# A hybrid S5 and Hyena encoder on one core: laying out and loading the constants and first spectra of the inverse transform anew

## The chip, the cores and the metric

The kernel runs on one core of one Trainium2 chip. The metric is the device time of one execution in microseconds; the median of three runs before the change is 1438.66 us (1438.37 to 1439.34). The trace is one profiled execution, and every start time below counts from its first instruction. TensorE (PE in the trace; PEld is its weight load), VectorE (DVE), ScalarE (ACT), GpSimd (POOL) and SyncE (SP) each run their own list of instructions in order; SP, ScalarE and GpSimd also issue the transfers (DMAs), and an issue that waits holds up what is behind it on that engine.

## The reference

One residual layer on `x` (1 x 1024 x 1024, float32): RMSNorm, one wide input projection, two token mixers side by side (a bidirectional S5 scan and a Hyena operator), a gated merge, an output projection, a residual add and a last RMSNorm. The change lies in the Hyena part:

```python
sc = conv_b
for j in range(HY_SHORT):
    sc = sc + pp[:, j:j + L] * conv_w[j]
v, x1, x2 = jnp.split(sc, HY_ORDER + 1, axis=-1)
kf = hyena_filters(L, w1, b1, freq, w2, b2, w3, decay)
z = v.astype(f32)
for o, g in enumerate((x1, x2)):
    zf = jnp.fft.rfft(z, n=2 * L, axis=1)
    conv = jnp.fft.irfft(zf * kf[:, o][None], n=2 * L, axis=1)[:, :L]
    z = g.astype(f32) * (conv + d[o].astype(f32) * z)
```

Everything is computed to float32 precision. TensorE gets it by splitting each operand in a high and a low part and adding three products (high-high, low-high, high-low).

## The kernel before, in words

The transforms are matmuls with constant matrices. Each of the two orders (o = 0, 1) has a way out and a way back.

The way out (`forward`, called through `fwd_pools`) takes four groups of 256 channels (cq). For each group it makes spectra for four frequency blocks, in the order jj = 0, 2, 1, 3: matmuls with the constants `zc` and `z0` into PSUM, sums and differences `ke` and `x` on VectorE, products `m` with the filter's spectrum `kt` (loaded by SP, two buffers) on VectorE, and a store to the scratch tensor `d_y` in device memory (`emit`, L775, issued by ScalarE).

The way back (`inverse`, L630) handles 128 channels at a time, eight times. For each it needs four spectra (j = 0, 2, 1, 3), each loaded back to a raw tile `yraw` by SP (`spectrum`, L621), split by ScalarE (high part, a cast) and VectorE (low part, a subtraction) into a tile `y`, and then 48 matmuls against the constants `ic` (high and low, four blocks each) and `icp` (the padded first block). ScalarE copies half of the PSUM result to `isn`, VectorE makes `pm` from both halves. In the first way back (`hy_inverse0`) GpSimd multiplies `pm` with a gate and forms a sum and a difference (L836 to L840), TensorE transposes the result (`store`, `to_time`), and it is stored for the second way out. There is one PSUM accumulator for it, so an inverse can't begin before the last one's result has been read.

Between the inverses TensorE works on projections of the normalised input. For the gates of the first way back there are eight, `x1(0)` to `x1(7)`: five are put ahead of the first inverse, and run among the matmuls of the last way out; the other three are cut in thirds (`proj_thirds`) and dealt between the inverses by the tuple (1, 2, 1, 1, 1, 2, 1, 0). Each projection's weights are loaded raw by SP (L508), cast and negated by ScalarE, and completed by a transfer of GpSimd that adds (L512).

Tiles live in pools, and pools are stacked from a left and a right end of the on-chip memory. When a pool is closed its room is given to the next one opened there; the first writer of a new tile then waits for the last reader of every old tile that its own tile overlaps. On the right side, above the gates, the way out has `fw_c` (`zc` 24 KB and `z0` 2 KB per partition), then `fw_w` (both `kt` 4 KB each, `eo2` 2 KB, `z` 16 KB) and `fw_t` (`m` 8 KB, then three tiles of 4 KB for `ke` and `x`). The way back has there `iv_c` (two `ic` tiles of 16 KB, `icp` 2 KB), and then the raw spectra, `y`, `isn` and `pm`. On the left, past the normalised input, lie three tiles `fv` of 4 KB, read by the transposes ahead of the way out. `load_ic` issues all nine loads on SP, ahead of the spectra.

The order on each engine is made by a planner that follows the program's order as priority and simulates when each instruction would be ready; `issue_after(i)` puts the instructions of a block behind instruction `i` on that instruction's engine, and `high_priority` moves them forward. Each inverse is put behind the last matmul of the projection before it (`self.summed`), each third behind the last matmul of an inverse (`self.rotated`).

Of the kernel before, what the change touches and what calls it, by code (L numbers as in the profile page):

```python
# [9 lines left out]
F = mybir.dt.float32  # L10
R = mybir.dt.float32r
# [89 lines left out]
class Trunk:  # L101
# [503 lines left out]
            V.tensor_tensor(out=o[:, 1], in0=self.minus(t), in1=self.minus(g), op=ALU.mult)  # L605
            V.tensor_tensor(out=z, in0=t[:, 0:1], in1=g[:, 0:1], op=ALU.mult)

    def load_ic(self, cp):
        nc, I = self.nc, self.staged
        self.ic = [cp.tile([128, 4, 1026], R, name=f"ic{i}") for i in range(2)]  # L610
        self.ic0 = cp.tile([128, 512], R, name="icp")
        nc.sync.dma_start(out=self.ic0.bitcast(F), in_=I["c_ic0"])
        for j in (0, 2, 1, 3):
            for i, sfx in enumerate(("hi", "lo")):
                nc.sync.dma_start(out=self.ic[i][:, j].bitcast(F), in_=I["c_ic_" + sfx][:, j])

    def inverse_start(self, o):
        self.iv_todo = [(o, cq, ct, j) for cq in range(4) for ct in range(2) for j in (0, 2, 1, 3)]
        self.iv_ready = []

    def spectrum(self):  # L621
        o, cq, ct, j = self.iv_todo.pop(0)
        raw = self.iv_r.tile([128, 2, 2, 128], F, name="yraw")
        self.nc.sync.dma_start(out=raw.rearrange("p a b c -> p (a b) c"),
                               in_=self.d_spec[o][cq, j][:, :, ct * 128:ct * 128 + 128])
        y = self.iv_y.tile([128, 2, 2, 2, 128], R, name="y")
        self.split(raw, y[:, 0], y[:, 1])
        self.iv_ready.append(y)

    def inverse(self, pi):  # L630

        nc = self.nc
        ps = pi.tile([128, 2, 512], F, name="iv")
        for nj, j in enumerate((0, 2, 1, 3)):
            while len(self.iv_ready) < self.iv_ahead and self.iv_todo:
                self.spectrum()
            y = self.iv_ready.pop(0)
            for par in range(2):
                for pqi in range(2):
                    cols, dst = (((slice(0, 258), ps[:, 0, 0:258]), (slice(514, 770), ps[:, 0, 256:512])),  # L640
                                 ((slice(258, 514), ps[:, 1, 0:256]),
                                  (slice(770, 1026), ps[:, 1, 256:512])))[par][pqi]
                    for a, b in ((0, 0), (0, 1), (1, 0)):
                        lhsT = y[:, a, par, pqi]
                        first = nj == 0 and pqi == 0 and a == 0 and b == 0
                        last = nj == 3 and pqi == 1 and a == 1
                        if first and par == 0:
                            nc.tensor.matmul(out=ps[:, 0], lhsT=lhsT, rhs=self.ic0, start=True, stop=False)
                        else:
                            self.rotated = nc.tensor.matmul(out=dst, lhsT=lhsT, rhs=self.ic[b][:, j, cols], start=first, stop=last)  # L650
        while len(self.iv_ready) < self.iv_ahead and self.iv_todo:
            self.spectrum()
        s = self.iv_w.tile([128, 2, 256], F, name="isn", bufs=1)
        nc.scalar.copy(out=s, in_=ps[:, :, 256:512])
        pm = self.iv_w.tile([128, 2, 512], F, name="pm")
        for a, op in enumerate((ALU.add, ALU.subtract)):
            nc.vector.tensor_tensor(out=pm[:, a].rearrange("p (b q) -> p b q", b=2), in0=ps[:, :, 0:256], in1=s, op=op)
        nc.vector.tensor_copy(out=pm[:, 0, 0:1], in_=ps[:, 0, 0:1])
        nc.vector.tensor_copy(out=pm[:, 1, 0:1], in_=s[:, 0, 0:1])
        return pm  # L660
# [96 lines left out]
    def fwd_pools(self, ctx, o):  # L757

        tc, nc = self.tc, self.nc
        mk = lambda n, b, **kw: ctx.enter_context(tc.tile_pool(reuse_waits="tile", name=f"{n}{o}", bufs=b, side="right", **kw))  # L760
        cp, wp, tp = mk("fw_c", 1), mk("fw_w", 1), mk("fw_t", 3)
        self.pf = mk("fw_p", 4, space=PSUM)
        self.load_zc(cp)
        self.d_spec[o] = self.dram.tile([4, 4, 128, 4, NCH], F, name=f"d_y{o}")

        class Pools:
            @staticmethod
            def tile(shape, dt, name, tag=None, bufs=None):
                if tag == "t4":
                    return tp.tile(shape, dt, name=name, tag=tag)  # L770
                if tag == "t8":
                    return tp.tile(shape, dt, name=name, tag=tag, bufs=1)
                return wp.tile(shape, dt, name=name, bufs=bufs)

        def emit(cq, jj, y):  # L775
            nc.scalar.dma_start(out=self.d_spec[o][cq, jj], in_=y.rearrange("p a b c -> p (a b) c"))

        return wp, lambda cq, z: self.forward(o, cq, z, Pools, self.pf, lambda jj, y: emit(cq, jj, y))

    def inv_pools(self, ctx, o, ny):  # L780
        tc = self.tc
        mk = lambda n, b, **kw: ctx.enter_context(tc.tile_pool(reuse_waits="tile", name=f"{n}{o}", bufs=b, side="right", **kw))
        self.load_ic(mk("iv_c", 1))
        self.iv_r, self.iv_y, self.iv_w = mk("iv_r", ny[0]), mk("iv_y", ny[1]), mk("iv_w", 2)
        self.iv_ahead = ny[1]

    def hy_v(self):

# [32 lines left out]
    def hy_inverse0(self):  # L821

        tc, nc = self.tc, self.nc
        self.d_z1 = self.dram.tile([4, 128, 2, 2048], F, name="d_z1")
        with ExitStack() as ctx:
# [2 lines left out]
            pi = ctx.enter_context(tc.tile_pool(reuse_waits="tile", name="iv_p", bufs=1, space=PSUM, side="right"))  # L828
            pt = ctx.enter_context(tc.tile_pool(reuse_waits="tile", name="iv_pt", bufs=2, space=PSUM, side="right"))
            gates, back = {}, {}  # L830
            self.inverse_start(0)

            def rotate(c):
                g = gates.pop(c)
# [13 lines left out]
            def x1(c):  # L848
                def use_x1(ps):
                    g = self.gates[c % len(self.gates)]  # L850
                    self.fold(self.conv(ps, 8 + c, "cv"), None, g)
                    gates[c] = g.rearrange("p a b c d -> p a (b c d)")
                return 16 + c, use_x1

            for c in range(5):
                self.proj(*x1(c))
            thirds = (t for c in range(5, 8) for t in self.proj_thirds(*x1(c)))
            for c, n in enumerate((1, 2, 1, 1, 1, 2, 1, 0)):
                with tc.issue_after(self.summed.ins):
                    rotate(c)  # L860
                if c:
                    store(c - 1)
                with tc.issue_after(self.rotated.ins):
                    for _ in range(n):
                        next(thirds)
# [470 lines left out]
    def inverse_tail(self, ctx):  # L1336

        self.inv_pools(ctx, 1, (6, 4))
        self.inverse_start(1)
        self.iv_p = ctx.enter_context(self.tc.tile_pool(reuse_waits="tile", name="iv_p1", bufs=2, space=PSUM, side="right"))  # L1340

    def hy_inverse1(self, zh, zl):
# [173 lines left out]
```

## Time and profile before

| what | us |
|---|---|
| median of three runs | 1438.66 |
| the profiled execution | 1442.31 |
| its span, first to last instruction | 1440.2 |
| TensorE busy | 1347.0 (94%) |
| VectorE busy | 1012.9 (70%) |
| ScalarE busy | 516.1 (36%) |
| GpSimd busy | 398.3 (28%) |

A matmul counts as busy from its start to its modelled end, and matmuls overlap, so a busy TensorE is not one at its peak; an idle one is idle. The first way out ends and the first way back begins between 840 and 900 us; the second pair does so between 1110 and 1170 us. Those two stretches, and the waits in them, are what the change touches.

### The profile page before, as it was taken

To read this page: it belongs to the slowest core of one execution; us is meant where nothing else is said; L and a number is where in the kernel's file an instruction comes from. 1 tells how busy PE (TensorE), PEld (TensorE's weight loads), DVE (VectorE), ACT (ScalarE), POOL (GpSimd) and SP (SyncE) were. 2 spreads that over 40 slices of the span, in tenths; PEclk is the share of its full clock that TensorE was granted. 3 is DMA by queue.
4 is the path that set the end of the run, shared out by engine and by line. 5 is a ranking of instruction groups with operands and counts; after the bars stand their busy time and mean duration, and the time that the engine had idled before them with its cause. 6 is when DMAs were issued, how large, how long until landed. Compare 5 with 4: busy or idle time off the path is not lost.

```text
span 1440.2 us, 19526 instructions
## 1 busy us (share of the span) xinstructions
PE 1347.0 (94%) x7219; PEld 1133.2 (79%) x7219; DVE 1012.9 (70%) x1938; ACT 516.1 (36%) x737; POOL 398.3 (28%) x331
## 2 busy tenths in 40 slices
PE   5888999999999999999999983999999989999997
PEld 3777798888888877887788873998888768978886
DVE  7999997698689878224499994663898734743632
ACT  5576663223323332442322221443222224522322
POOL 3766775000000001132112100553022223332222
PEclk8898999999999999999999996999999999999999
DMA  8221225864794644567965658569787897766331
GB/s 275 92 75 74 81 116 135 207 159 132 200 272 113 135 122 95 150 166 200 327 188 166 185 168 263 176 205 306 235 273 249 261 262 228 212 181 155 130 111 68
DMA packets 188619, 257.24 MB, mean 179 GB/s; under 512 B 23069, under 2 KB 144153, under 8 KB 185788
## 3 DMA queue, kind: packets, MB, share of 16 engines
q1 hardware_dynamic: 149212, 153.69, 34.4%
q0 software_dynamic: 11520, 39.85, 14.6%
q10 hardware_dynamic: 27792, 62.45, 12.1%
q8 instruction: 57, 0.93, 0.3%
q14 instruction: 38, 0.31, 0.1%
HBM read 147.49 MB, written 76.82 MB: 156 GB/s over the span
## 4 chain that ended last, share of the span: by engine, by line
PE 63%; DVE 15%; DMA 9%; issue 2%; ACT 1%; POOL 1%; SPq 0%; ACTq 0%; DVEq 0%; POOLq 0%
PE pps L556 38%; PE ops L1417 6%; PE iv L650 5%; DMA yraw<-d_y 3%; DMA zc<-c_zc_lo_d 2%; PE po L404 2%; PE pps L536 2%; PE fwo L701 2%; DMA d_y<-x 2%; PE pe L414 1%; PE fwe L701 1%; DVE st L1249 1%; DVE st L1247 1%; PE zt L686 1%; DMA ic<-c_ic_lo_d 1%
## 5 line engine op out<-in xcount | busy, mean ns | idle before, releaser
L512 POOL DMA_DIRECT2D wlo<-wraw x76 | 66.2, 871 | 709.1 <-ACT wlo L511 523.0
L556 PE MATMUL pps<-xh,whi 128*128 128x512 f32 x848 | 216.6, 403 | 4.0 <-DVE cv L581 4.0
L556 PE MATMUL pps<-xl,whi 128*128 128x512 f32 x848 | 212.5, 397 | 0.0
L556 PE MATMUL pps<-xh,wlo 128*128 128x512 f32 x848 | 210.1, 396 | 0.0
L556 PEld LDWEIGHTS pps<-xh,whi 128*128 128x128 f32 x848 | 159.9, 192 | 41.4 <-ACT wlo L511 3.6
L556 PEld LDWEIGHTS pps<-xh,wlo 128*128 128x128 f32 x848 | 157.9, 188 | 36.8
L556 PEld LDWEIGHTS pps<-xl,whi 128*128 128x128 f32 x848 | 157.3, 188 | 36.2 <-issue 0.2
L510 ACT CAST whi<-wraw 128x1024 fp32r<-128x1024 f32 (+1 forms) x76 | 74.7, 983 | 284.2 <-PE pps L556 245.1
L404 PE MATMUL po<-sh,fo 128*128 128x256 f32 x512 | 100.3, 290 | 6.8 <-DVE sh L111 5.6
L650 PEld LDWEIGHTS iv<-ic,y 128*128 128x128 f32 x752 | 93.3, 191 | 3.5 <-DVE y L113 1.6
L650 PE MATMUL iv<-ic,y 128*128 128x256 f32 (+1 forms) x752 | 94.7, 284 | 1.2 <-DVE y L113 1.0
L404 PEld LDWEIGHTS po<-sh,fo 128*128 128x128 f32 x512 | 83.4, 195 | 9.6 <-DVE sh L111 6.6
L113 DVE TENSOR_TENSOR y<-yraw,y 128x512 fp32r<-128x512 f32 x64 | 54.4, 870 | 47.1 <-ACT y L109 38.7
L357 POOL TENSOR_TENSOR acc<-acc,sq 128x512 f32<-128x512 f32 x56 | 76.9, 1373 | 21.8 <-ACT sq L342 19.9
L511 ACT ACTIVATE wlo<-whi 128x1024 fp32r<-128x1024 f32 (+1 forms) x76 | 74.9, 985 | 20.4 <-PE pps L556 20.2
L579 DVE SCALAR_TENSOR_TENSOR cv<-pps,cw,cv 128x1023 f32<-128x1023 f32 x24 | 30.7, 1280 | 67.5 <-ACT cv L578 67.5
L404 PE MATMUL po<-sl,fo 128*128 128x256 f32 x256 | 73.9, 289 | 0.0
L109 ACT CAST y<-yraw 128x512 fp32r<-128x512 f32 x64 | 39.6, 620 | 81.2 <-DMA yraw<-d_y 45.5
L578 ACT ACTIVATE cv<-pps,cb,cw 128x1024 f32<-128x1024 f32 x24 | 29.0, 1208 | 70.4 <-PE pps L556 50.4
L404 PEld LDWEIGHTS po<-sl,fo 128*128 128x128 f32 x256 | 50.1, 196 | 1.0 <-DVE sl L113 0.2
L333 PE MATMUL g<-w3h,ha 128*128 128x512 f32 x64 | 33.0, 515 | 19.2 <-DVE e L338 17.4
L701 PE MATMUL fwo<-z,zc 128*128 128x256 f32 x384 | 49.7, 283 | 0.0
(443 smaller groups left out, 2765.4 us busy)
## 6 DMA issues: line engine op xcount, KB each, us to landing
wlo<-wraw POOLq DMA_DIRECT2D x64, 512.0 KB, 5.7
wraw<-w_in SPq DMA_DIRECT2D x56, 512.0 KB, 5.3
kspec<-ko SPq DMA_DIRECT2D x32, 512.0 KB, 2.9
kt<-kspec SPq DMA_DIRECT2D x32, 512.0 KB, 4.7
d_y<-x ACTq DMA_DIRECT2D x32, 512.0 KB, 3.7
yraw<-d_y SPq DMA_DIRECT2D x64, 256.0 KB, 5.7
d_m<-cv ACTq DMA_DIRECT2D x16, 512.0 KB, 2.7
d_z<-z ACTq DMA_DIRECT2D x8, 1024.0 KB, 4.1
```

Of the source, the lines that this page charges most:

```text
L109: nc.scalar.copy(out=hi, in_=src)
L113: e.tensor_tensor(out=lo, in0=src, in1=hi, op=ALU.subtract)
L333: nc.tensor.matmul(out=ps, lhsT=ha[:, tsl], rhs=w3h, start=True, stop=False)
L357: nc.gpsimd.tensor_tensor(out=acc, in0=acc, in1=sq, op=ALU.add)
L404: nc.tensor.matmul(out=po[:, part], lhsT=fo[a][:, 12 * (jj % 2) + b], rhs=sd[4 + i][d][:, part], start=n == 0 and part == 0, stop=n == 11 ...
L510: nc.scalar.copy(out=hi, in_=raw)
L511: nc.scalar.activation(out=lo, in_=hi, func=AF.Copy, scale=-1.0)
L512: nc.gpsimd.dma_start(out=lo, in_=raw, accum_op=ALU.add)
L556: self.summed = nc.tensor.matmul(out=ps[:, hf * 512:hf * 512 + 512], lhsT=w[:, kc], rhs=part(x, kc, hf), start=a == 0 and p == 0 and kc == ...
L650: self.rotated = nc.tensor.matmul(out=dst, lhsT=lhsT, rhs=self.ic[b][:, j, cols], start=first, stop=last)
L701: nc.tensor.matmul(out=out, lhsT=zc[a][:, b], rhs=z[:, :, d, zi], start=start and n == 0, stop=stop and n == 3 * len(prods) - 1)
L1417: nc.tensor.matmul(out=pss[cs.start][:, 0:cs.stop - cs.start], lhsT=m[:, kc, ts], rhs=w[kc][:, cs], start=kc == 0 and p == 0, stop=kc == 7 ...
```

## The change

The two `ic` tiles are cut in eight, one for each block j and part, and with `icp` make nine tiles, which are allocated in a set order: six (blocks 1, 2, 0) in the pool opened first, then `ic[1, 3]` with the first `pm` tile and, in the first way back, a pad of 464 words, then four fixed `y` tiles, then `isn` and the second `pm`. In the first way back the raw spectra, `icp` and `ic[0, 3]` go to the left side, over the `fv` tiles; in the second they follow on the right. `y` and `pm` become fixed tiles that are used in turn.

In the first way back GpSimd issues eight of the nine loads and ScalarE the ninth (`ic[1, 3]`); in the second all are issued by SP, as before. Right behind the loads, the first four spectra are loaded and split at a raised priority; in the first way back the low parts of these four are made by GpSimd. The stores of the last group's spectra jj = 1 and 3 move from ScalarE's queue to SP's, for both orders. In the first way back, projection `x1(4)` (with the weight load that it starts) is put behind the constants' loads on GpSimd, and the thirds are dealt as (2, 1, 1, 1, 1, 2, 1, 0).

```diff
--- before.py
+++ after.py
@@ -605,16 +605,8 @@
             V.tensor_tensor(out=o[:, 1], in0=self.minus(t), in1=self.minus(g), op=ALU.mult)
             V.tensor_tensor(out=z, in0=t[:, 0:1], in1=g[:, 0:1], op=ALU.mult)
 
-    def load_ic(self, cp):
-        nc, I = self.nc, self.staged
-        self.ic = [cp.tile([128, 4, 1026], R, name=f"ic{i}") for i in range(2)]
-        self.ic0 = cp.tile([128, 512], R, name="icp")
-        nc.sync.dma_start(out=self.ic0.bitcast(F), in_=I["c_ic0"])
-        for j in (0, 2, 1, 3):
-            for i, sfx in enumerate(("hi", "lo")):
-                nc.sync.dma_start(out=self.ic[i][:, j].bitcast(F), in_=I["c_ic_" + sfx][:, j])
-
     def inverse_start(self, o):
+        self.iv_n = self.iv_c = 0
         self.iv_todo = [(o, cq, ct, j) for cq in range(4) for ct in range(2) for j in (0, 2, 1, 3)]
         self.iv_ready = []
 
@@ -623,8 +615,9 @@
         raw = self.iv_r.tile([128, 2, 2, 128], F, name="yraw")
         self.nc.sync.dma_start(out=raw.rearrange("p a b c -> p (a b) c"),
                                in_=self.d_spec[o][cq, j][:, :, ct * 128:ct * 128 + 128])
-        y = self.iv_y.tile([128, 2, 2, 2, 128], R, name="y")
-        self.split(raw, y[:, 0], y[:, 1])
+        y = self.iv_y[self.iv_n % self.iv_ahead]
+        self.split(raw, y[:, 0], y[:, 1], lo_eng="pool" if o == 0 and self.iv_n < 4 else "dve")
+        self.iv_n += 1
         self.iv_ready.append(y)
 
     def inverse(self, pi):
@@ -647,12 +640,13 @@
                         if first and par == 0:
                             nc.tensor.matmul(out=ps[:, 0], lhsT=lhsT, rhs=self.ic0, start=True, stop=False)
                         else:
-                            self.rotated = nc.tensor.matmul(out=dst, lhsT=lhsT, rhs=self.ic[b][:, j, cols], start=first, stop=last)
+                            self.rotated = nc.tensor.matmul(out=dst, lhsT=lhsT, rhs=self.ic[b, j][:, cols], start=first, stop=last)
         while len(self.iv_ready) < self.iv_ahead and self.iv_todo:
             self.spectrum()
         s = self.iv_w.tile([128, 2, 256], F, name="isn", bufs=1)
         nc.scalar.copy(out=s, in_=ps[:, :, 256:512])
-        pm = self.iv_w.tile([128, 2, 512], F, name="pm")
+        pm = self.iv_pm[self.iv_c % 2]
+        self.iv_c += 1
         for a, op in enumerate((ALU.add, ALU.subtract)):
             nc.vector.tensor_tensor(out=pm[:, a].rearrange("p (b q) -> p b q", b=2), in0=ps[:, :, 0:256], in1=s, op=op)
         nc.vector.tensor_copy(out=pm[:, 0, 0:1], in_=ps[:, 0, 0:1])
@@ -773,16 +767,46 @@
                 return wp.tile(shape, dt, name=name, bufs=bufs)
 
         def emit(cq, jj, y):
-            nc.scalar.dma_start(out=self.d_spec[o][cq, jj], in_=y.rearrange("p a b c -> p (a b) c"))
+            q = nc.sync if cq == 3 and jj % 2 else nc.scalar
+            q.dma_start(out=self.d_spec[o][cq, jj], in_=y.rearrange("p a b c -> p (a b) c"))
 
         return wp, lambda cq, z: self.forward(o, cq, z, Pools, self.pf, lambda jj, y: emit(cq, jj, y))
 
     def inv_pools(self, ctx, o, ny):
-        tc = self.tc
-        mk = lambda n, b, **kw: ctx.enter_context(tc.tile_pool(reuse_waits="tile", name=f"{n}{o}", bufs=b, side="right", **kw))
-        self.load_ic(mk("iv_c", 1))
-        self.iv_r, self.iv_y, self.iv_w = mk("iv_r", ny[0]), mk("iv_y", ny[1]), mk("iv_w", 2)
+
+
+        tc, nc, I = self.tc, self.nc, self.staged
+        mk = lambda n, b, side="right": ctx.enter_context(
+            tc.tile_pool(reuse_waits="tile", name=f"{n}{o}", bufs=b, side=side))
+        far = "left" if o == 0 else "right"
+        cp, kp, yp = mk("iv_c", 1), mk("iv_k", 1), mk("iv_y", 1)
+        tile = lambda p, i, j: p.tile([128, 1026], R, name=f"ic{i}{j}")
+        self.ic = {(i, j): tile(cp, i, j) for j in (1, 2, 0) for i in range(2)}
+        self.ic[1, 3] = tile(kp, 1, 3)
+        self.iv_pm = [kp.tile([128, 2, 512], F, name="pm0")]
+        if o == 0:
+            kp.tile([128, 464], F, name="icpad")
+        self.iv_y = [yp.tile([128, 2, 2, 2, 128], R, name=f"y{i}") for i in range(ny[1])]
+        self.iv_w = mk("iv_w", 2)
+        self.iv_pm.append(self.iv_w.tile([128, 2, 512], F, name="pm1", bufs=1))
+        self.iv_r = mk("iv_r", ny[0], far)
+        fp = mk("iv_f", 1, far)
+        self.ic0 = fp.tile([128, 512], R, name="icp")
+        self.ic[0, 3] = tile(fp, 0, 3)
         self.iv_ahead = ny[1]
+        eng = nc.gpsimd if o == 0 else nc.sync
+        load = lambda e, i, j: e.dma_start(out=self.ic[i, j].bitcast(F), in_=I["c_ic_" + ("hi", "lo")[i]][:, j])
+        eng.dma_start(out=self.ic0.bitcast(F), in_=I["c_ic0"])
+        for j in (0, 2, 1):
+            for i in range(2):
+                self.rotating = load(eng, i, j)
+        load(eng, 0, 3)
+        with tc.high_priority(offset=60):
+            load(nc.scalar if o == 0 else nc.sync, 1, 3)
+        self.inverse_start(o)
+        with tc.high_priority(offset=60):
+            for _ in range(self.iv_ahead):
+                self.spectrum()
 
     def hy_v(self):
 
@@ -828,7 +852,6 @@
             pi = ctx.enter_context(tc.tile_pool(reuse_waits="tile", name="iv_p", bufs=1, space=PSUM, side="right"))
             pt = ctx.enter_context(tc.tile_pool(reuse_waits="tile", name="iv_pt", bufs=2, space=PSUM, side="right"))
             gates, back = {}, {}
-            self.inverse_start(0)
 
             def rotate(c):
                 g = gates.pop(c)
@@ -852,10 +875,12 @@
                     gates[c] = g.rearrange("p a b c d -> p a (b c d)")
                 return 16 + c, use_x1
 
-            for c in range(5):
+            for c in range(4):
                 self.proj(*x1(c))
+            with tc.issue_after(self.rotating.ins):
+                self.proj(*x1(4))
             thirds = (t for c in range(5, 8) for t in self.proj_thirds(*x1(c)))
-            for c, n in enumerate((1, 2, 1, 1, 1, 2, 1, 0)):
+            for c, n in enumerate((2, 1, 1, 1, 1, 2, 1, 0)):
                 with tc.issue_after(self.summed.ins):
                     rotate(c)
                 if c:
@@ -1336,7 +1361,6 @@
     def inverse_tail(self, ctx):
 
         self.inv_pools(ctx, 1, (6, 4))
-        self.inverse_start(1)
         self.iv_p = ctx.enter_context(self.tc.tile_pool(reuse_waits="tile", name="iv_p1", bufs=2, space=PSUM, side="right"))
 
     def hy_inverse1(self, zh, zl):
```

## Rows read from the trace of the kernel before

**Rows 1.** Busy tenths in 40 slices of 36 us, TensorE (page)

```profile
PE   5888999999999999999999983999999989999997
```

**Rows 2.** Windows: busy us of PE, PEld, DVE, ACT, POOL; clock, DMA share, GB/s

```profile
840.00:860.00 20.00, 19.05 (x98) 15.78 (x96) 19.43 (x26) 5.17 (x5) 0.86 (x1) 1.00 0.59 172
860.00:880.00 20.00, 0.00 (x0) 0.00 (x0) 11.96 (x17) 1.24 (x2) 0.86 (x1) 0.58 0.81 252
880.00:900.00 20.00, 12.54 (x76) 11.54 (x77) 6.93 (x12) 5.44 (x9) 1.96 (x1) 0.74 0.79 247
900.00:920.00 20.00, 20.00 (x137) 18.33 (x136) 13.05 (x19) 10.36 (x16) 10.80 (x11) 1.00 0.48 135
...
980.00:1000.00 20.00, 20.00 (x92) 16.24 (x91) 3.18 (x6) 8.67 (x11) 2.94 (x5) 1.00 1.02 359
```

**Rows 3.** Chain of waits, in order of time: start us, us, what

```profile
845.76 13.31 PE pps L556 x57
...
888.25 6.63 PE iv L650 x47
...
913.02 5.59 PE iv L650 x47
...
1045.79 3.09 DVE m L735
```

**Rows 4.** Timeline around the way back's start: start, us, engine, line, operation

```profile
842.72 3.04 PE L701 MATMUL fwo<-z,zc 128*128 128x256 f32 x24
...
858.17 1.23 DVE L735 TENSOR_TENSOR m<-x,kt 128x1024 f32<-128x1024 f32 x1
...
869.80 0.34 SPq L615 DMA_DIRECT2D ic<-c_ic_hi_d  x1
...
871.64 0.69 DVE L740 TENSOR_TENSOR x<-m 128x512 f32<-128x512 f32 x1
...
886.78 0.62 ACT L109 CAST y<-yraw 128x512 fp32r<-128x512 f32 x1 [25.54 <-DMA yraw<-d_y]
...
887.46 0.79 PE L648 MATMUL iv<-icp,y 128*128 128x512 f32 x1 [28.40 <-ACT y L109]
```

**Rows 5.** Timeline from the first inverse's end to the second's start

```profile
894.72 3.90 PE L536 MATMUL pps<-xh,whi 128*128 128x512 f32 x16
...
896.49 1.28 DVE L657 TENSOR_TENSOR pm<-iv,isn 128x512 f32<-128x512 f32 x2
...
898.46 0.39 PE L648 MATMUL iv<-icp,y 128*128 128x512 f32 x1
```

**Rows 6.** DMA queues (MB, share of 16 engines); issues (KB, us to landing)

```profile
q0 software_dynamic: 11520, 39.85, 14.6%
...
yraw<-d_y SPq DMA_DIRECT2D x64, 256.0 KB, 5.7
```

**Rows 7.** GpSimd by line and shape: count, busy us, mean ns, idle before

```profile
L512 POOL DMA_DIRECT2D wlo<-wraw x76 | 66.2, 871 | 709.1 <-ACT wlo L511 523.0 <-ACT ts L1192 46.4 <-DVE ez L1375 30.6
...
L836 POOL TENSOR_TENSOR pm<-pm,gate 128x1024 f32<-128x1024 f32 x6 | 14.4, 2402 | 59.0 <-DVE pm L659 59.0
...
L837 POOL TENSOR_TENSOR gate<-pm 128x512 f32<-128x512 f32 x6 | 7.7, 1287 | 0.5
...
L317 POOL TENSOR_TENSOR w3l<-w,w3h 128x512 fp32r<-128x512 f32 x1 | 1.3, 1262 | 8.3 <-ACT w3h L316 8.3
```

**Rows 8.** Timeline of one GpSimd operation, VectorE full, then VectorE idle

```profile
1111.14 6.39 POOL L604 TENSOR_TENSOR vf<-cv,sg 128x512 f32<-128x512 f32 x1 [4.68 <-issue]
...
1155.74 2.15 POOL L604 TENSOR_TENSOR vf<-cv,sg 128x512 f32<-128x512 f32 x1 [0.75 <-DMA wlo<-wraw]
```

**Rows 9.** Timeline around the second way back's start

```profile
1138.95 0.34 SPq L615 DMA_DIRECT2D ic<-c_ic_hi_d  x1
...
1163.68 0.80 PE L648 MATMUL iv<-icp,y 128*128 128x512 f32 x1 [4.57 <-ACT y L109]
```

**Rows 10.** Chain of waits, end of the second forward's matmuls

```profile
1110.20 1.43 PE fwo L701 x12
```

## The prediction

> **What bounds the kernel now.** I read four views, from coarse to fine. The slices of the page show TensorE busy to nine tenths almost everywhere after the first slices, with one deep hole at slice 25 of 40 [rows 1]. The windows around it say what the hole is: from 860 to 880 us TensorE does nothing, VectorE works 12 of 20 us, and in 880 to 900 TensorE is back with a clock that fell [rows 2]. So the kernel is bound by TensorE, and the time to be had is a stretch in which it stands still. The chain of waits crosses the hole in this order: last x1 projection until 859.1, VectorE's tail, constants, spectra, inverse transform [rows 3]. The timeline gives the releases [rows 4]: TensorE's last forward matmul ends at 845.8; VectorE runs behind it and ends its last forward operation at 872.3; the constants go out only at 869.8, when the last m that reads kt is done; the spectra queue behind them on SP; the first cast starts at 886.8 and TensorE restarts at 887.46, after 28.40 us. The restart is also slow: the first inverse (47 matmuls) takes 6.63 us against 5.59 later, and its first matmul 0.79 against 0.39 [rows 3 to 5], because the clock granted in 860 to 880 was 0.58 [rows 2]. Cost of the lower clock: 1.0 + 0.4 = 1.4 us.
>
> **The change part by part, first way back.** What I sum is the start of the second inverse, rotate(1): 898.46 before [rows 5].
>
> Constants. Before, two tiles of 16 KB lie over z0, zc, eo2 and both kt, so they wait for the last m. After, six tiles (24.6 KB) lie over zc and z0 (26 KB), free when TensorE's last forward matmul ends, 845.8; ic0 and ic[0,3] lie where the fv tiles were, read last by the transposes ahead of that forward; ic[1,3] lies over the kt of jj=1, read last by the m that ends at 859.4 [rows 4]. Eight go through GpSimd: 8 x 0.87 us of issue [rows 7], 7.0 us, from an engine busy 0.86 of 20 us there [rows 2]: hidden. If that cover were gone, it is 7.0 us at most on the first ones.
>
> Their landing. 4.2 MB of constants (8 x 513 KB and 256 KB) and 1 MB of spectra. Where the engines are full (980 to 1000, share 1.02) they move 359 GB/s; in 840 to 860 other transfers already move 172 [rows 2]. That leaves 187, so 4.2 MB from 846 on are in at 868.5, say 870 with the last issue (an estimate from these two rows; nothing here waits for another load to land). From the same rate: the first pair (1 MB, j=0) at about 852, in good time; j=2 at 858, j=1 at 864, j=3 at 870. If the queue of GpSimd ran at what q0 shows over the span (39.85 MB in 14.6% of 1440 us, 190 GB/s with all engines its own) [rows 6] and got only the 0.41 of the engines that are free, the last pair would land at 878. I take 870: plain loads make up the windows' rows, and most of q0's bytes are the weights' low halves, which are added to what is there.
>
> Spectra. The raw tiles move to the fv room and can load before the last forward ends; y lies over z and eo2, free with that forward's last matmul and the last ke behind it. Four casts on ScalarE (0.62 us each [rows 4], ScalarE busy 5 of 20 us [rows 2]) hide. The four subtractions move to GpSimd: 128x512 fp32r there took 1.26 us [rows 7], 5.0 us together, 8 to 12 us of GpSimd with the issues, done by about 858 if nothing stretches them. Upper bound: a GpSimd operation on 128x512 beside a full VectorE took 6.39 us, the same one beside an idle VectorE 2.15 [rows 8]; four at 6.39 end at about 874.
> The lockout: an m takes 1.23 us [rows 4], but 3.09 at 1045.8, where GpSimd multiplied [rows 3], so both sides pay. The Trainium skill (SBUF — State Buffer, "Who interferes with whom") says why: a VectorE operation with both inputs in SBUF and a GpSimd operation that reads SBUF lock each other out for a whole instruction. By that rule VectorE's tail would grow by at most the four subtractions, and the sum below would be 880 in place of 879.
>
> rotate(0). Its two PSUM banks last held po of jj=2 and jj=1, whose x come before the m at 858.17, so they are free. It starts at x1(4)'s end plus a cast and semaphores, about 860 (not 887.46), and ends when j=3 is in, about 871.5, of which 5.6 is work.
>
> What is late next. Two thirds of a projection now follow it (before: one), 3.74 us each [rows 5]: 871.5 + 7.5 = 879. rotate(1) also needs the single iv accumulator emptied. isn lies over m, so ScalarE's copy waits for VectorE's end, 872.3; from the inverse's last matmul to the end of pm it was 2.9 us (894.88 to 897.77 [rows 3, 5]): 875 (880 with 5 us of lockout). And it needs spectra 4 to 7: their loads are on SP, where two of the last d_y stores now are too, the second waiting for VectorE until 872.3; behind it a spectrum is in at 872.9 + 5.7 = 878.6 [rows 6] and cast at 879; ahead of it, some 10 us earlier. All three conditions end within 875 to 880; I take 879. Off ScalarE's queue the stores can't hold the casts there until 872; on SP they hold spectra and a weight, and weights are loaded two ahead, six thirds, 22 us of matmuls.
>
> Sum: rotate(1) starts at 879 with one third more done: 898.46 - (879 - 3.74) = 23.2 us. Ends: 17 if the subtractions or loads are late as above, 29.8 (28.40 + 1.4) if nothing is late at all. The weight of x1(5) is queued on GpSimd behind the constants; its low half is needed in the third that follows rotate(1), after 880: no cost. After rotate(1), TensorE goes on as before, without gaps [rows 2], and the rest of the kernel moves forward whole.
>
> **Second way back.** SP still loads. The six tiles over zc now wait for TensorE's last forward matmul (1111.6 [rows 10]), not for the m before 1138.95 [rows 9]; the raw tiles move under the x tiles, which wait for the last d_y stores. TensorE stood 4.57 us there, for a first cast, at 1163.7 [rows 9]. Best: 4.6 saved. Worst: SP stands for a late room and holds the weights queued behind it; with 1139 to 1112 as the longest stand, 27 us, and 22 us of weights ahead, 5 us are lost and the 4.6 stay. I take 2 saved, about halfway between 4.6 and nothing, since the transfers move to a stretch that is busy too.
>
> **Total.** 23.2 + 2 = 25 us. The profiled execution took 1442.31 (span 1440.2), so 1417 for such an execution; the median shown is 3.65 less, 1438.66, hence 1413.5.
>
> **Rivals.**
> (A) The inputs of rotate(0) come late: loads at q0's rate (last pair 878) or subtractions stretched to 6.39 us (874 plus the last quarter). rotate(0) ends at 877 to 879.5, rotate(1) starts at 885 to 887, gain 15 to 17: 1421 to 1424. For: [rows 6, 8]. Against: the issue of a load by GpSimd took its 0.87 us on the mean over stretches with VectorE full too, and the loads of the first two quarters have time in hand.
> (B) The rooms are not free early: something over which constants or y now lie is released only by the last m, as before. Then loads go out at 869.8, only the queueing on SP goes, two constants are in at about 876, rotate(1) at 889, gain 13: 1425.5. For: kt and m stay in use to the end. Against: sizes, as worked out above.
> (C) Nothing is late and the second stall goes too: 29.8 + 4.6 = 34: 1404.
> (D) Slower: GpSimd becomes the bound of the way back. Each rotation asks of it 2.40 + 1.29 + 1.29 (the other difference) + 0.87 = 5.9 us [rows 7]; TensorE needs 5.59 + 9/8 x 3.74 = 9.8 per rotation. If VectorE, now a tail behind, stays full and stretches each of these threefold (6.39 against 2.15), a rotation takes 17.6; eight lose 62 us, less 23 gained: 1438.66 + 39 = 1478. It decides from a stretch of 2.15 on: 5.9 x 2.15 = 12.7 = 9.8 + 23.2/8. Against: VectorE is busy 13 of 20 us in 900 to 920 [rows 2] and the same operations took 1.29 there.
>
> **How the numbers follow.** Forecast (gain 19 to 30 in all, 1409 to 1420) 0.62; A 0.16; B 0.09; C 0.08; D and the like of it 0.05. The predicted time is the forecast's, 1413.5. The range 1405.5 to 1424.5 holds the forecast, most of A and most of C and leaves out B and D: about 0.8. What a measurement of this kernel can tell from no change is some 0.2%, 2.9 us. Faster by more: forecast, A, C and nearly all of B, 0.92; within: 0.03, out of B; slower: D, 0.05.
>
> **What would show it.** In the profile after: constants issued by GpSimd from about 846 and not 869.8; first spectra issued before 846, their four subtractions on GpSimd near 1.3 us; TensorE's wait before the first inverse under 3 us, rotate(0) ending near 871 with waits for j=3 inside, a wait of some us ahead of rotate(1) at most; granted clock of 860 to 880 near 1.00; the start of the second way back's first inverse without 4.57 us of waiting. I am wrong if the first inverse starts after 865, if the subtractions last 5 us or more, if VectorE's last forward operation ends after 878, or if new waits of more than 5 us appear after the way back.

## The result, and the profile after

Four runs of the changed kernel: median 1415.78 us (1413.96 to 1416.76). Four of the kernel before: 1438.51 (1435.61 to 1439.34). The ratio is 0.9844, interval [0.9827, 0.9861]: 22.7 us faster, forecast 25. The time was 1413.5 forecast, 1415.8 measured. The profiled execution of the changed kernel took 1413.96 us, its span is 1412.2.

The page of the changed kernel, TensorE's busy tenths and granted clock in 40 slices of 35.3 us. Of the hole of slice 25 [rows 1] a 7 is left in slice 25 here, with the only lower clock of the second half:

```profile
PE   5888899999999999999999997999999999999997
...
PEclk9999999999999999999999998999999999999999
```

The same stretch closely, timeline of the changed kernel (start, us, engine, line, operation, in brackets the idle time ahead of it and what ended it):

```profile
838.98 3.04 PE L695 MATMUL fwo<-z,zc 128*128 128x256 f32 x24
...
842.32 0.55 POOL L798 DMA_DIRECT2D ic<-c_ic_hi_d  x1 [15.36 <-PE fwo L695]
...
853.30 0.69 DVE L724 TENSOR_TENSOR x<-ke,fwo 128x512 f32<-128x512 f32 x1 [2.94 <-DMA d_y<-x]
...
856.20 1.20 ACT L578 ACTIVATE cv<-pps,cb,cw 128x1024 f32<-128x1024 f32 x1 [3.54 <-DVE x L734]
...
859.16 0.33 ACTq L798 DMA_DIRECT2D ic<-c_ic_lo_d  x1
859.53 2.18 ACT L109 CAST y<-yraw 128x512 fp32r<-128x512 f32 x4 [1.18 <-DVE u L602]
860.20 0.80 PE L641 MATMUL iv<-icp,y 128*128 128x512 f32 x1 [4.88 <-ACT y L109]
860.23 11.11 POOL L113 TENSOR_TENSOR y<-yraw,y 128x512 fp32r<-128x512 f32 x4 [0.71 <-ACT y L109]
...
862.76 5.36 PE L643 MATMUL iv<-ic,y 128*128 128x258 f32 x24 [1.56 <-POOL y L113]
...
868.50 3.38 DVE L731 TENSOR_TENSOR m<-m 128x512 f32<-128x512 f32 x2
...
869.69 3.17 PE L643 MATMUL iv<-ic,y 128*128 128x258 f32 x22 [1.57 <-POOL y L113]
...
872.52 0.68 DVE L734 TENSOR_TENSOR x<-m 128x512 f32<-128x512 f32 x1
872.70 3.90 PE L536 MATMUL pps<-xh,whi 128*128 128x512 f32 x16
873.24 0.34 SPq L771 DMA_DIRECT2D d_y<-x  x1
...
879.53 0.62 ACT L109 CAST y<-yraw 128x512 fp32r<-128x512 f32 x1 [0.63 <-DMA yraw<-d_y]
880.06 0.58 ACT L647 COPY isn<-iv 128x512 f32<-128x512 f32 x1
...
882.28 0.47 PE L641 MATMUL iv<-icp,y 128*128 128x512 f32 x1 [1.96 <-DVE pm L653]
```

Its windows (busy us of PE, PEld, DVE, ACT, POOL; granted clock, DMA share, GB/s) answer to those of [rows 2]:

```profile
855.00:860.00 5.00, 0.32 (x2) 0.00 (x0) 5.00 (x8) 2.62 (x3) 0.87 (x1) 0.76 0.89 250
860.00:866.00 6.00, 4.25 (x17) 3.74 (x18) 6.00 (x10) 1.71 (x4) 5.77 (x3) 0.50 0.94 234
866.00:874.00 8.00, 6.43 (x39) 5.82 (x39) 7.17 (x8) 0.00 (x0) 5.33 (x2) 0.89 0.62 186
```

How to compare the times of two traces: the changed kernel's last forward matmul ends at 842.02, that of before at 845.76 [rows 4]. TensorE's matmuls up to there are the same in both; the changed loads begin at 818.68, and by 762 us the two executions already differ by those 3.74 us. So times below are counted from that matmul's end ("at +18.2").

| counted from the last forward matmul | before | forecast | after |
|---|---|---|---|
| rotate(0) starts | +41.7 | +14.2 | +18.2 |
| rotate(0) ends | +49.1 | +25.7 | +30.8 |
| VectorE's last forward operation ends | +26.6 | +26.6 | +31.2 |
| rotate(1) starts (after: with a third more done) | +52.7 | +33.2 | +40.3 |

With the third that is done in addition, 3.74 us [rows 5], the gain at the second inverse is 52.7 + 3.74 - 40.3 = 16.2 us, not 23.2. The second way back gave more than forecast: its first inverse no longer waits at all, where it waited 4.57 us [rows 9]. From the last matmul of the second way out (which ends at 1111.6 before, at 1090.5 after) to the end of the last matmul the two traces have 320.9 and 314.2 us, 6.7 us less. In the changed kernel's timeline these are TensorE's only waits from 990 us to 1300 us:

```profile
1202.32 3.15 PE L643 MATMUL iv<-ic,y 128*128 128x258 f32 x24 [1.67 <-DVE y L113]
...
1223.64 3.14 PE L643 MATMUL iv<-ic,y 128*128 128x258 f32 x24 [0.68 <-DVE y L113]
...
1247.69 3.98 PE L556 MATMUL pps<-ozh,whi 128*128 128x512 f32 x16 [1.08 <-DVE ez L1402]
```

### The profile page after: what moved, and what is told of

It reads as the page before. It is cut to its first block, busy times and chain, and to the rows that moved or that the text cites. A ratio compares the mean times of both kernels' runs of the same rounds, so it can differ in the third digit from the quotient of the medians.

```text
span 1412.2 us, 19536 instructions
## 1 busy us (share of the span) xinstructions
PE 1346.7 (95%) x7219; PEld 1135.9 (80%) x7219; DVE 1014.1 (72%) x1934; ACT 515.1 (36%) x737; POOL 416.6 (29%) x343
## 4 chain that ended last, share of the span: by engine, by line
PE 72%; DVE 18%; DMA 5%; issue 3%; ACT 1%; POOL 1%; SPq 0%; ACTq 0%; DVEq 0%; POOLq 0%
PE pps L556 43%; PE ops L1441 6%; PE iv L643 5%; PE po L404 4%; PE fwo L695 3%; DMA zc<-c_zc_lo_d 2%; PE pe L414 2%; PE pps L536 2%; DVE rsq_h L125 2%; DVE e L338 1%; PE fwe L695 1%; DMA d_y<-x 1%; DVE st L1274 1%; PE zt L680 1%; DVE st L1272 1%
```

## Experiments

My theory after reading the two traces: the first way back is held at three places in a row, all of them order in a queue, not missing data. (1) rotate(0) starts late since the first casts stand on ScalarE behind x1(4)'s work, which stands behind a d_y store that waits for VectorE, and behind the issue of ic[1,3]. (2) GpSimd's subtractions are slow beside VectorE. (3) rotate(1) waits for a chain of its own: spectra 5 to 7 on SP behind the last d_y store, then their casts, then isn and pm. If so, mending (1) and (2) without (3) buys nothing. The edits are shown against the changed kernel, main lines only ("..." stands for lines not shown). The times of e1 to e4 stand beside nine runs of the kernel before (median 1440.30), f1 to f4 beside seven (median 1439.72).

### e1 and e2: each way back alone

e1 keeps the first way back as before and changes the second; e2 the other way round. In each, the queue of the stores goes with its way back; in e1 `x1(4)`, the thirds and the engine of the subtractions are also as before.

```
     def inv_pools(self, ctx, o, ny):
+        if o == 0:                                    # e1; in e2: o == 1
+            return self.inv_pools_old(ctx, o, ny)     # tiles, loads and spectra as before
...
```

> The second way back as changed, the first as before the change. My prediction gave this part 2 us: 1436.5. Reading the two traces against each other (TensorE's waits from the second way back on fall from 8.2 to 3.4 us, with a lower clock after one of them) I now expect 5 to 7 us less than before the change: 1431.5 to 1433.5. Rival: the part gives nothing of its own and the waits went because everything ahead had shifted: 1438.5.

> The first way back as changed, the second as before the change. My prediction gave this part 23 us: 1415.3. Reading the traces (last transposes of the first way back 14.9 us earlier, counted from the end of the first way out) I now expect 15 to 17 us: 1421.5 to 1423.5. If both parts add up, this gain and that of the run with the second part alone sum to 22.7.

e1: 1436.14 us, ratio 0.9963 [0.9949, 0.9977], that is 5.3 us by the ratio (4.2 by the medians). By the ratio this lies in the theory's band, by the medians between it and the prediction's 2 us. e2: 1422.62, ratio 0.987 [0.9854, 0.9886], 18.7 us. That is above the 15 to 17 that I expected of it and below the 23 of the prediction; in its trace the second inverse of the first way back gains 16.5 us (it starts at +39.9), at the lower end of the interval (16.4 to 21.0), and what makes up the rest no run shows. The product of both ratios, 0.9833, lies in the interval of the whole: the two halves add up. Timeline of e2: its first two inverses wait as in the whole change, and the old wait of the second way back is there:

```profile
860.46 0.79 PE L641 MATMUL iv<-icp,y 128*128 128x512 f32 x1 [4.66 <-ACT y L109]
...
882.45 0.47 PE L641 MATMUL iv<-icp,y 128*128 128x512 f32 x1 [1.85 <-DVE pm L653]
...
1145.82 0.79 PE L641 MATMUL iv<-icp,y 128*128 128x512 f32 x1 [4.26 <-ACT y L109]
```

Window of e1 where the kernel before has that wait; there the same ten microseconds held 6.32 us of matmuls at a granted clock of 0.83:

```profile
1160.00:1170.00 10.00, 10.00 (x45) 8.04 (x44) 2.52 (x5) 4.17 (x5) 0.88 (x1) 1.00 1.08 362
```

So these 5.3 us belong to the second way back: the whole wait of 4.57 and the lower clock behind it. Of the small waits around it some grew and some shrank, none by over 0.8 us.

TensorE's order has changed there too. Before, the two opening matmuls of the second way back's first inverse stood in the middle of the projections, 47.5 us behind the second way out (there they waited from 1159.11 to 1163.68), and the other 46 followed only behind the last projection of the input:

```profile
1202.92 5.60 PE L650 MATMUL iv<-ic,y 128*128 128x258 f32 x46
```

In e1 and in the changed kernel the whole first inverse stands behind the last projection, 84 us behind the second way out. Timeline of the changed kernel:

```profile
1135.32 0.62 ACT L109 CAST y<-yraw 128x512 fp32r<-128x512 f32 x1 [3.40 <-DMA yraw<-d_y]
...
1174.36 0.39 PE L641 MATMUL iv<-icp,y 128*128 128x512 f32 x1
```

Its first cast ends 45.4 us behind the second way out, some 2 us ahead of the place where TensorE stood before; and at the new place even the old cast (1163.02, 51.4 us behind) would have come some 30 us in time. Earlier data and the new order each do away with the wait; no run tells them apart.

### e3: the four subtractions on VectorE

```
-        self.split(raw, y[:, 0], y[:, 1], lo_eng="pool" if o == 0 and self.iv_n < 4 else "dve")
+        self.split(raw, y[:, 0], y[:, 1], lo_eng="dve")
```

> The changed kernel with the four early low parts subtracted by VectorE and not by GpSimd. If VectorE's queue sets the pace (my theory), the four subtractions stand behind its tail, the first inverse ends at 877 or later in place of 872.9 and the time grows by 2 to 4 us, to 1418 to 1420. Rival: the lockout costs more than it gives (the four took 11.1 us on GpSimd and stretched one pair of VectorE's operations by 2.1); then the tail ends 2 us earlier and the time falls by 1 to 3 us.

1419.08 us, ratio 0.9848 [0.9832, 0.9863]. By the ratio it is the same as the change (0.6 us apart); the median lies in the theory's band, beside a kernel before that is 1.8 us above. Neither side is shown by times alone. The trace shows what each placing costs. Timeline of e3:

```profile
871.10 1.28 DVE L731 TENSOR_TENSOR m<-m 128x512 f32<-128x512 f32 x2
872.30 0.68 DVE L113 TENSOR_TENSOR y<-yraw,y 128x512 fp32r<-128x512 f32 x1
873.03 7.59 PE L643 MATMUL iv<-ic,y 128*128 128x258 f32 x46 [9.59 <-DVE y L113]
```

On VectorE the first subtraction comes when its forward work is all but through, and TensorE waits 9.59 us. But VectorE's pair of 128x512 operations takes 1.28 us, where in the changed kernel, beside GpSimd's subtraction, the same pair took 3.38. What GpSimd gives TensorE it takes from VectorE. Counted from e3's last forward matmul (844.99), VectorE's forward work ends 2.0 us earlier than in the change (+29.2), as the rival had it; the first inverse ends 4.8 us later (+35.6), and so the second starts 2.7 us later (+42.9), without a wait of its own, as the theory had it.

### e4: first spectra ahead of everything else on ScalarE

The casts are put ahead of x1(4)'s work and of the issue of ic[1,3]; so that no store stands ahead of them, the last group's stores jj=1 to 3 of the first way out go through SP. The issue of ic[1,3] is moved behind the first spectra in both ways back.

```
-            with tc.issue_after(self.rotating.ins):
+            with tc.issue_after(self.rotating.ins), tc.issue_after(self.cast.ins):
                 self.proj(*x1(4))
...
-            q = nc.sync if cq == 3 and jj % 2 else nc.scalar
+            q = nc.sync if cq == 3 and (jj > 0 if o == 0 else jj % 2) else nc.scalar
...
-            load(nc.scalar if o == 0 else nc.sync, 1, 3)      # ahead of the first spectra
+            load(nc.scalar if o == 0 else nc.sync, 1, 3)      # behind them
```

> The changed kernel with ScalarE's four casts of the first spectra put ahead of its work for x1(4) and x1(5) and ahead of the load of ic[1,3], and with all three late stores of the last group on SP. The first inverse should start at about 856 and not 860.2, without the 4.9 us wait and the halved clock, and its subtractions run from 847 on. Theory: the second inverse does not follow, since spectra 5 to 7 stand on SP behind the last store (873.2) and isn behind their casts; it stays near 881 and the time within 1.5 us of 1415.8. Rival: the late start is what the first way back lost; then the second inverse moves up too and the time falls by 4 to 6 us, to 1410 to 1412.

1419.33 us, ratio 0.9848 [0.9827, 0.987]: no gain, as the theory had it (the median is 3.5 us above 1415.8, beside a kernel before that is 1.8 above; by the ratio it is the same). Timeline of e4 (its last forward matmul ends at 842.77):

```profile
846.01 2.17 ACT L619 CAST y<-yraw 128x512 fp32r<-128x512 f32 x4
846.70 6.41 POOL L621 TENSOR_TENSOR y<-yraw,y 128x512 fp32r<-128x512 f32 x4 [0.49 <-ACT y L619]
...
863.41 1.78 PE L645 MATMUL iv<-ic,y 128*128 128x258 f32 x11 [2.78 <-DMA ic<-c_ic_lo_d]
...
868.54 0.32 SPq L773 DMA_DIRECT2D d_y<-x  x1
868.95 5.52 SPq L616 DMA_DIRECT2D yraw<-d_y  x5
...
878.06 0.62 ACT L619 CAST y<-yraw 128x512 fp32r<-128x512 f32 x1 [0.31 <-DMA yraw<-d_y]
...
878.59 0.58 ACT L649 COPY isn<-iv 128x512 f32<-128x512 f32 x1
...
880.82 0.76 PE L643 MATMUL iv<-icp,y 128*128 128x512 f32 x1 [6.80 <-DVE pm L655]
```

The first inverse now starts at +13.1 without a wait, its subtractions are done before it, it waits 2.78 us for ic[1,3] alone, and ends 8.4 us earlier than in the change (+22.4). And the second starts at +38.1: the gain has turned into a wait of 6.80 us for pm. One sees the chain in the rows: the store at 868.54, three spectra behind it, the last cast at 878.06, isn right behind, pm, the matmul.

### f1 and f2: the chain of the second inverse

f1 is e4 with one store, jj=3, on GpSimd. f2 is f1 with isn laid over the padding's room, so that it no longer lies over m.

```
-            q = nc.sync if cq == 3 and (jj > 0 if o == 0 else jj % 2) else nc.scalar
+            q = (nc.gpsimd if jj == 3 and o == 0 else nc.sync) if cq == 3 and (jj > 0 if o == 0 else jj % 2) else nc.scalar
```

```
-            kp.tile([128, 464], F, name="icpad")
+        self.iv_s = None if o else kp.tile([128, 2, 256], F, name="isn")     # f2
```

> The casts-first version once more, with the last d_y store (jj=3) issued by GpSimd instead of SP, so that spectra 5 to 7 stand on SP behind the store of jj=2 alone. My theory: what held the second inverse at 880.8 in the casts-first version was SP's order (raws 5 to 7 behind the store at 868.5, hence the casts to 878 and isn behind them on ScalarE). Now casts 4 to 7 end by 868, isn goes as soon as VectorE's last m frees its room (868 to 870), pm ends at 872 to 873 and the second inverse starts at 872 to 875: 5.5 to 8 us below the change, ratio to the kernel before 0.979 to 0.981 (1408 to 1411 where the change takes 1415.8). Rival: another lock stands right behind (VectorE's queue, the constants of j=3, the lower granted clock after the earlier start), the second inverse starts after 878 and the ratio stays within 0.9835 to 0.9855.

> As the version with the last store aside, and isn laid over the room of the padding instead of over m, so that it no longer waits for VectorE's last forward operations. My theory: pm stands behind those operations in VectorE's own queue, so an earlier isn buys little: ScalarE's copy (0.6 us) drops out ahead of pm, 0 to 1.5 us below the version with the last store aside. Rival: isn over m was the condition that counted: 3 us or more below it. A third outcome: the other layout lets the second way back's first constant be loaded among the first way back's spectra on SP, and a wait there holds raws back: 2 us or more above it.

f1: 1408.93 us (1408.17 to 1412.16), ratio 0.979 [0.9773, 0.9807]. That is 30.2 us below the kernel before by the ratio, and its interval lies wholly below the change's. f2: 1411.93, ratio 0.9805 [0.979, 0.9819]: not below f1. Timeline of f1 (last forward matmul ends at 842.18):

```profile
862.49 1.59 PE L645 MATMUL iv<-ic,y 128*128 128x258 f32 x11 [2.44 <-DMA ic<-c_ic_lo_d]
...
862.98 12.73 SPq L616 DMA_DIRECT2D yraw<-d_y  x8
...
867.76 0.58 POOL L773 DMA_DIRECT2D d_y<-x  x1 [14.68 <-DVE x L736]
...
869.85 0.63 ACT L619 CAST y<-yraw 128x512 fp32r<-128x512 f32 x1 [0.16 <-DMA yraw<-d_y]
...
870.38 0.57 ACT L649 COPY isn<-iv 128x512 f32<-128x512 f32 x1
...
873.43 1.28 DVE L653 TENSOR_TENSOR pm<-iv,isn 128x512 f32<-128x512 f32 x2
...
874.92 0.47 PE L643 MATMUL iv<-icp,y 128*128 128x512 f32 x1 [3.39 <-DVE pm L655]
```

The spectra leave at 862.98 and not behind 868.54, the last cast ends at 870.5 and not 878.7, the second inverse starts at +32.7 against +38.1 in e4 and +40.3 in the change. The last transposes of this way back begin 119.2 us after the last forward matmul against 125.9 in the change: 6.7 us, which makes most of the difference of the ratios (0.0054, 7.8 us). Expected was a start of 872 to 875; it was 874.92. f1 has the casts first as well; what the store's move alone would give, no run shows. Timeline of f2:

```profile
871.38 0.58 ACT L649 COPY isn<-iv 128x512 f32<-128x512 f32 x1
...
874.53 1.28 DVE L653 TENSOR_TENSOR pm<-iv,isn 128x512 f32<-128x512 f32 x2
...
876.02 0.47 PE L643 MATMUL iv<-icp,y 128*128 128x512 f32 x1 [1.99 <-DVE pm L655]
```

isn isn't earlier and the start is the same (+33.0): in both it stands behind the last cast in ScalarE's queue, and pm behind four subtractions in VectorE's. So isn over m was not the condition that counted. By the median f2 is 3.0 us above f1, by the ratio 2.2, which is what the third outcome named; the intervals overlap. In the trace the second way back's first constants do leave among the spectra (873.99 and 876.51 on SP), but the last transposes begin no later than in f1 (+119.0 against +119.2). What is later is the end of the second way out's matmuls, by 2.6 us, of which 1.94 are a wait for VectorE that f1 hasn't; why it is there stays open.

### f3: the same constants, loaded by SP

```
-        eng = nc.gpsimd if o == 0 else nc.sync
+        eng = nc.sync
```

> The changed kernel with its constants of the first way back issued by SP, as before, instead of GpSimd; rooms and order as in the change. My theory: on SP they queue behind kt loads that wait for VectorE, so the constants of j=0 start after 853 instead of at 843, and weights and the last kt behind them are late: the first inverse starts at 863 to 868 instead of 860.2, the whole is 3 to 8 us above the change (ratio 0.9865 to 0.990). Rival: the queue that loads them doesn't matter, since the first inverse waits for the casts anyway: within 1.5 us of the change (ratio 0.9833 to 0.9855).

1418.46 us, ratio 0.9849 [0.983, 0.9868]: by the ratio the rival's case, the same as the change, and my theory of 3 to 8 us fell, though the median is 2.7 us above 1415.8. Timeline of f3 (last forward matmul ends at 844.84):

```profile
844.87 0.32 SPq L798 DMA_DIRECT2D ic<-c_ic_hi_d  x1
...
865.34 0.80 PE L641 MATMUL iv<-icp,y 128*128 128x512 f32 x1 [7.21 <-ACT y L109]
...
885.63 0.39 PE L641 MATMUL iv<-icp,y 128*128 128x512 f32 x1
```

I had thought that the constants would stand behind kt loads; they left at +0.03, as early as on GpSimd (+0.3), since the room, not the queue, had held them. Behind them a weight is late, and the first inverse starts at +20.5, 2.3 us later than in the change. (865.34 lies in the theory's 863 to 868 only because this execution came to the stretch 2.8 us later.) But the second starts at +40.8 against +40.3: the first has slack. By the Trainium skill (DMA: Bandwidth & Descriptors, "SWDGE vs HWDGE vs iDMA") plain transfers belong on SP's or ScalarE's queue, GpSimd's being for those that accumulate or cast. Here neither was the better by the time: one issue took 0.54 us on GpSimd and 0.32 to 0.65 on SP.

### f4: one third, not two, between the first two inverses

```
-            for c, n in enumerate((2, 1, 1, 1, 1, 2, 1, 0)):
+            for c, n in enumerate((1, 2, 1, 1, 1, 2, 1, 0)):
```

> The changed kernel with the thirds dealt as before: one, not two, between the first inverse and the second. My theory: the second inverse's start is set by pm, so the third that is missing there leaves a wait of 1.96 + 3.74 = 5.7 us, and the third done later fills no wait: 3 to 5.5 us above the change (ratio 0.9863 to 0.988), more than 3.74 where the longer wait lowers the granted clock. Rival: the third fills a wait further on (before the first transposes): within 1.5 us of the change.

1421.42 us, ratio 0.9878 [0.986, 0.9896], 4.9 us above the change by the ratio. Timeline of f4:

```profile
882.15 0.77 PE L641 MATMUL iv<-icp,y 128*128 128x512 f32 x1 [5.49 <-DVE pm L653]
...
882.72 7.21 PE L643 MATMUL iv<-ic,y 128*128 128x258 f32 x47
```

The start stays where pm puts it; the missing third has become a wait of 5.49 in place of 1.96, and after the longer wait the 47 matmuls take 7.21 us against 5.79 in the change. So 4.9 us of the change's 22.7, a third of 3.74 and the clock with it, come from the way the thirds are dealt, and they need a wait to fill. The theory of 3 to 5.5 us holds.

## Why the prediction was right, and where its steps were not

**Right.** The rooms are free early: two constants of the left side left at 819, and the first of the six over zc and z0 0.3 us after the last forward matmul (842.32 against 842.02), so rival B is out. The third moved forward fills the wait ahead of the second inverse (f4). GpSimd did not bind the way back: after rotate(1) its waits come to 0.45 us, so rival D is out. The whole came 2.3 us from the forecast, but that is luck in good part, since two errors go against each other: first way back 18.7 us (e2) against 23.2, second 5.3 (e1) against 2.

**Failed: "It starts at x1(4)'s end plus a cast and semaphores."** The cover named for the casts, ScalarE busy 5 of 20 us, is a share of time, not an order. x1(4)'s matmuls end at 855.32, and from there ScalarE's queue held the casts for 4.2 us: 0.88 until x1(4)'s activation starts at 856.20, behind the store of jj=2, which waits for VectorE; 2.15 for that activation and the low half of the next weight; and 1.18 for the issue of ic[1,3], which waits for VectorE too (the prediction had its room released at 859.4, but had not put its issue ahead of the casts). Price: +18.2 against +14.2. e4 and f1 show it: with the casts first there is no wait. The Trainium skill (PSUM — Partial Sum Buffer, "Engine vs sequencer instructions") calls ScalarE's queue strictly first in, first out; the trace agrees (casts at 859.53, right behind the issue at 859.16).

**Failed: "128x512 fp32r there took 1.26 us [rows 7], 5.0 us together".** The four took 11.11 us beside a VectorE that was full from 858 to 870, and 6.41 and 6.97 where they came earlier (e4, f1). The upper end, 6.39 each, was too high, the lower too low. TensorE waited for them 1.56 and 1.57 us, and they cost VectorE 2.1 us (3.38 against 1.28 in e3). This is the lockout of [rows 3, 8], which I had weighed and given 1 us. With 2.94 us in which VectorE waits for a d_y store to land, its last forward operation ends 4.6 us late. The engines' share is 1.03 around there (419 GB/s in 850 to 855), so I take it that the constants hold that store up; no run isolates it.

**Failed: "ends when j=3 is in".** In the change no matmul waits for a constant. rotate(0) takes 12.7 us: 5.6 of work at full clock, 3.1 of waits for GpSimd, and 3.9, the rest, most of it because the granted clock was 0.50 from 858 to 866, in and after the wait of 4.88: 24 matmuls took 5.36 us there, where 47 of the second inverse took 5.79. Where the casts come first (e4, f1), it is ic[1,3] indeed that is late, by 2.8 and 2.4 us. The loads were faster than the sum had them: a constant landed 11.4 us after its issue at most, so the last of GpSimd's was in by about +15, where the sum had the pair of j=1 at +18 (864). And the 878 of rival A does not follow from the figures beside it: 0.41 of 190 GB/s is 78, at which 4.2 MB take 54 us, until 900.

**Failed, and the one that set the time: "All three conditions end within 875 to 880".** The three were named, and the last of them decided; its sum was short. I ended it with one spectrum cast. But isn stands behind the casts of spectra 5 to 7, all three, on ScalarE, and pm behind isn on VectorE. From the store's issue on: first cast after 4.1 us (forecast 5.7), to the end of the last cast 2.8 more, isn and pm 2.1: 882.3. With the store itself 4.1 us late this makes the 7.0 us between +33.2 and +40.3. That it was this chain and not the inputs of rotate(0) is what e4 (first inverse done 8.4 us earlier, second starting 2.2 earlier) and f1 (one store moved, another 5.3 us) show.

**Mis-sized: "I take 2 saved".** Halving the best case was a guess about busy transfers. In the changed kernel the constants leave from 1090.56 on (six by 1096.3, ic[1,3] at 1122.11), right behind the second way out's matmuls, the first cast starts 44.8 us behind them and not 51.4, and the whole 4.57 us went, with the lower clock of 1160 to 1170. But TensorE also asks for that cast 36 us later than before, an order that the prediction did not foresee, so that the wait is gone is shown, and that the earlier constants did it is not.

Rival A (late inputs, 1421 to 1424) described rotate(0) better than my forecast did, and its start of rotate(1), 885 to 887, is what was measured (+40.3 is 886.0 on the clock of before). But it had rotate(0)'s end set that start, and f3 shows how little the inputs were worth: 2.3 us later, same time. Its total missed because it left out the second way back, as that of rival B does. Of the signs that I had set for being right, four did not come: subtractions near 1.3 us, a wait of under 3 us before the first inverse (4.88), an end of rotate(0) near 871 with waits for j=3 inside (876.6 on the clock of before, with none), and a granted clock near 1.00 from 860 to 880 (0.80). Of those for being wrong, one came: a subtraction of over 5 us (the longest took 5.73). The first inverse (+18.2, 863.9 on the clock of before) and VectorE's end (+31.2, 876.9) stayed just inside theirs, of 865 and 878.

## What to carry to other kernels

When a stall goes, write down the next start as the maximum of its conditions, and follow each of them through every queue to the last instruction that the start needs, not to the first: here the second inverse hung on the third spectrum, a copy and an addition behind one store. An engine's busy share says nothing about when a given instruction of it can run; for each instruction that is moved forward, look at what stands ahead of it in its own queue and what that waits for, DMA issues included. Then mend the chain that ends last: the first inverse done 8.4 us earlier bought nothing (e4), and with one store moved off that chain as well the kernel was 7.8 us below the change (f1). And when a wait has gone, look whether the instruction that waited still stands at its place in the order, before the change's data get the credit.

## What the runs showed of the hardware

GpSimd's plain loads took 0.54 us each to issue, not the 0.87 of its accumulating ones [rows 7]. The same 128x512 subtraction on GpSimd took from 1.28 us to 5.73 in one row of four. And the granted clock of the change was 0.50, the lower of its two levels (1.2 GHz), from 858 to 866: the end of TensorE's wait of 4.88 us and 6 us of broken work behind it. In f1 a wait of 2.44 us that followed full work left it at 1.00 (from 863 to 875 too), and in the five microseconds after one of 3.39 it was 0.66. Windows of f1:

```profile
855.00:863.00 8.00, 5.56 (x44) 5.22 (x43) 7.93 (x13) 3.85 (x4) 0.00 (x0) 1.00 0.48 163
...
875.00:880.00 5.00, 5.00 (x29) 4.96 (x30) 0.60 (x1) 0.97 (x2) 4.92 (x4) 0.66 1.03 229
```
